# A two-layer decoder trunk on one core: another weight tile on the second queue, constants loaded later, early inputs stored without gaps, and a new hand-laid order

## The chip, the core and the metric

The kernel runs on one core of a Trainium2 chip. Its engines work side by side, each through its own instruction queue: PE (TensorE, matmuls; the profile shows its weight loads apart, as PEld), DVE (VectorE), ACT (ScalarE), POOL (GpSimd) and SP (SyncE), which issues nearly all transfers; ACT issues three. The metric is the device time of one execution in microseconds (us). Before the change the median of three runs is 358.94 us (358.47 to 359.08).

## What is computed

One sequence of 256 tokens of width 1,024 goes through two layers in float32. Layer 0 is block-sparse attention (with 256 tokens there is one block, so it is causal attention over 16 heads of 64), layer 1 is attention with a compressed, a selected and a window branch. Each layer has one input projection that also gives a SiLU gate, an output projection, and a gated per-layer embedding:

```
for i in range(DEPTH):                       # DEPTH = 2
    h = rms_norm(x, norm_gain[i])
    x = x + (moba_layer if i == 0 else nsa_layer)(h, ...)
    gate = sigmoid(rms_norm(x, ple_gate_gain[i]) @ ple_w_gate[i])
    x = x + gate * (p[i] @ ple_w_proj[i])

def moba_layer(h, w_in, q_gain, k_gain, w_out, pos):
    q, k, v, z = split(h @ w_in, 4)          # 1024 columns each
    q, k = rope(rms_norm(q, q_gain), pos), rope(rms_norm(k, k_gain), pos)
    return (attention(q, k, v) * silu(z)) @ w_out
```

## The kernel before

**Split matmuls.** The product of a float32 weight tile and the activations is made of three matmuls of type float32r. ACT (or DVE) copies a raw weight tile to `hi`, rounded; DVE subtracts, `lo = raw - hi`. The activation tile is split likewise, into the two halves of a tile `a`. Then PE adds hi x hi, hi x lo and lo x hi up in PSUM (`mul`, line 544). So a weight tile must be loaded, copied by ACT and subtracted by DVE before PE can use it whole; the matmuls with `hi` can run while `lo` is made.

**The start of the program.** The first unit of work is the queries of heads 0 to 7, `c0` to `c7`: one tile of 128 x 512 weights for each of the eight k-tiles of x (128 features each). Beside them run the first four k-tiles of the keys of the same heads, `d0` to `d3`, from the same activations. Each tile is two token halves of three matmuls of 512 columns, six in all; `c0` is loaded in two halves of 256 columns and takes twelve of half the width. `x0` to `x7` are the steps that load a k-tile of x (line 892) and split it, scaled by the gain; `w:c0` and so on load and split weights (lines 898 and 949); `c0`, `d0` and so on are the matmuls (lines 918 and 954). Steps `a.1` to `a.7` square the x tiles for the norm (ACT) and add the squares (DVE); `consts` loads the first constants and the gains of the heads, from which `tq` and `tk` make tables on DVE. Twenty matmuls on a constant (line 870) run first, while nothing has landed.

SP issues most transfers. ACT issues three before its first computation: the gains `gain_in`, the second half of c0's weights, and a third one, kept in the variable `second` (lines 883 and 884), which is `c1`.

**What sets the order.** The kernel is written as named steps. `PROGRAM` (line 25) is a list of step names, an order found by a search outside the kernel; it tells the order in which the steps are recorded and in which buffers are handed out. `Plan.schedule` (line 272) then deals the recorded operations to the engines: of those that are ready, each engine takes the one that can start first by a table of costs, and on equal times the one recorded first; a plain copy may go to ACT or DVE. For transfers this table holds an issue time, a lag and a rate by time of landing (`ISSUE, LAG, RATE`, line 242), and at most eight may be open (line 244). `hold` (line 262) keeps an operation until another one has been dealt; `BEHIND` (line 54) names the weight steps behind which the first constants and the rest of them are held. The instructions of each engine then run strictly in that order on the chip, each waiting on semaphores. All of them are issued from line 408, so every row of the profile carries that line, and tiles are told apart by name.

Raw tiles of the early steps lie in the five buffers `tmp` (shared with the squares of the norm and other short-lived values) or, from the fifth k-tile on, in pairs in the seven buffers `raw`; `hi` and `lo` have five buffers each, and `mm` is the PSUM of the projections.

Of the kernel before, what the change touches and what calls it, by code (L numbers as in the profile page):

```python
# [13 lines left out]
P = 128  # L14
T = 256
D = 1024
KT = 8
# [7 lines left out]
PROGRAM = ("x0 w:c0 x1 w:c1 w:d0 c0 x3 d0 x5 w:d1 c1 x2 consts w:c2 x4 w:d2 a.1 w:c3 c2 c3 x6 x7 w:c5 a.3 w:c4 c4 w:d3 a.5  "  # L25
# [28 lines left out]
BEHIND = "d0 k.2"  # L54
# [56 lines left out]
class Plan:  # L111
# [130 lines left out]
    ISSUE, LAG, RATE = 450.0, 2250.0, ((5000.0, 255.0), (9000.0, 340.0), (1e9, 400.0))  # L242
# [187 lines left out]
def trunk(ctx: ExitStack, tc: tile.TileContext, a, out):  # L430
# [28 lines left out]
    def load_consts(lo, hi):  # L459
        nc.sync.dma_start(cst[:, lo:hi], a["cst"][:, lo:hi])  # L460
# [258 lines left out]
    def tail(i, oT, pvs, zin, xz, norm):  # L719
# [21 lines left out]
        def load_p():  # L741
            pT = tmp("p").rearrange("p (k t) -> p k t", k=2)
            nc.sync.dma_start(pT, a["p"][:, i])
            for k in range(2):
                px[k] = split_act(pT[:, k])
# [130 lines left out]
    uq0 = Unit(a["moba_in"][0], False, x0)  # L876
    uq0.ps = [bank("mm", 4) for _ in range(2)]

    nc.sync.dma_start(xT[:, 0], a["x"][:, 0])
    halves = [load(a["moba_in"][0, 0, :, 0:256], 256, True)]  # L880
    since = len(nc.ops)
    nc.scalar.dma_start(gain_in, a["gain_in"])
    halves.append(load(a["moba_in"][0, 0, :, 256:512], 256, True, nc.scalar))
    second = load(a["moba_in"][0, 0, :, 512:1024], 512, True, nc.scalar)
# [7 lines left out]
    def first_x(k):  # L892
        if k:
            nc.sync.dma_start(xT[:, k], a["x"][:, k])
        x0[k] = split_act(xT[:, k], ng[:, 0, k:k + 1], k == 0)
        lows[k] = len(nc.ops) - 1

    def first_w(k):
# [4 lines left out]
        c0, raw = 512 * (k % 2), second if k == 1 else None  # L903
        if k >= 4:
# [4 lines left out]
            nc.sync.dma_start(raw, a["moba_in"][0, k // 2, :, c0:c0 + 512])  # L909
        since = len(nc.ops)  # L910
        uq0.w[k] = split(a["moba_in"][0, k // 2, :, c0:c0 + 512], (1, 512), small=k < 4, raw=raw)
# [525 lines left out]
def _arrays(i):  # L1437
    import numpy as np

    def c(v):  # L1440
        return np.ascontiguousarray(v)

    def feat(v):
        return c(v.reshape(KT, P, T).transpose(1, 0, 2))
# [92 lines left out]
```

## Time and profile before

| what | value |
|---|---|
| median of three runs | 358.94 us |
| profiled execution | 358.19 us |
| its span, first to last instruction | 356.4 us |
| PE busy | 349.5 us, 98% |
| weight loads busy | 305.6 us, 86% |
| DVE busy | 323.6 us, 91% |
| ACT busy | 276.8 us, 78% |
| granted TensorE clock | 1.000 |
| read from memory | 57.46 MB, 164 GB/s over the span |

A row of the timeline reads: start in us, length in us, engine, line, operation, the tiles written and read, shapes, how many are merged in the row, and in brackets the idle time before it and what ended it. A row of the groups has busy time and mean length after the bar. A row of the transfers gives size and the us from issue to landing. The profiled execution is 0.75 us shorter than the median of the runs. The end of a matmul is modelled, and the next one starts before it.

### The profile page before, as it was taken

Reading aid. Unit: us, or ns where it says so; the run is one execution under the profiler, and the core shown is the slowest. Engines: PE = TensorE matmul, PEld = TensorE weight load, DVE = VectorE, ACT = ScalarE, POOL = GpSimd, SP = SyncE. Lnnn points to the kernel's source line nnn. Section 1 sums busy time; section 2 is a strip of 40 time slices with the busy share of each in tenths; the row PEclk is TensorE's granted clock in tenths of the full one; section 3 lists DMA queues with packets and bytes.
Section 4 is the critical chain, followed back from the end, with each engine's and each line's share of the span. In section 5 each row is a group of like instructions: output and inputs, shape, how many; then the busy total and the mean of one; then the engine's idle time right before and its main releaser. Section 6 shows DMA issues by size and latency. Waiting matters only on the chain.

```text
span 356.4 us, 6657 instructions
## 1 busy us (share of the span) xinstructions
PE 349.5 (98%) x2315; PEld 305.6 (86%) x2315; DVE 323.6 (91%) x789; ACT 276.8 (78%) x613; POOL 28.0 (8%) x22
## 2 busy tenths in 40 slices
PE   7999999999999999999999999999999999999995
PEld 5788788989999888999889999877998888888884
DVE  3999899999999989889999999999999999979715
ACT  4875599999999986556854789979989999926721
POOL 1013403005000000000003300012000000000000
PEclk9999999999999999999999999999999999999999
DMA  7999376554534315653554865347653211352003
GB/s 219 318 410 387 124 255 231 176 179 166 160 109 145 123 59 164 203 171 114 166 183 142 269 237 179 124 161 259 232 157 102 95 59 62 91 183 81 0 2 118
DMA packets 20769, 58.94 MB, mean 165 GB/s; under 512 B 2560, under 2 KB 5632, under 8 KB 20736
## 3 DMA queue, kind: packets, MB, share of 16 engines
q1 hardware_dynamic: 20160, 58.04, 48.3%
q10 hardware_dynamic: 576, 0.48, 0.4%
q8 instruction: 18, 0.29, 0.3%
q14 instruction: 15, 0.12, 0.1%
HBM read 57.46 MB, written 1.05 MB: 164 GB/s over the span
## 4 chain that ended last, share of the span: by engine, by line
PE 93%; DVE 2%; ACT 2%; DMA 2%; issue 0%; DVEq 0%; ACTq 0%
PE mm L408 68%; PE tr L408 14%; PE s L408 10%; DMA xT<-in_x 1%; DMA gain_in<-in_gain_in 1%; DVE lo L408 1%; ACT hi L408 0%; DVE hl L408 0%; DVE pc L408 0%; DVE big L408 0%; ACT hl L408 0%; ACT sm L408 0%; ACT pt L408 0%; ACT vcB L408 0%; ACT tmp L408 0%; DVE tmp L408 0%
## 5 line engine op out<-in xcount | busy, mean ns | idle before, releaser
L408 PE MATMUL mm<-hi,a 128*128 128x512 f32 (+2 forms) x448 | 128.2, 375 | 1.9 <-ACT sqacc L408 1.2
L408 ACT ACTIVATE hi<-raw 128x1024 fp32r<-128x1024 f32 (+2 forms) x98 | 97.5, 1006 | 32.8 <-PE mm L408 21.6
L408 DVE TENSOR_TENSOR lo<-raw,hi 128x1024 fp32r<-128x1024 f32 (+2 forms) x98 | 112.4, 1160 | 6.9 <-ACT hi L408 6.6
L408 PE MATMUL mm<-a,hi 128*128 128x256 f32 (+1 forms) x512 | 107.8, 300 | 0.0
L408 PEld LDWEIGHTS mm<-hi,a 128*128 128x128 f32 x448 | 79.3, 189 | 15.7 <-ACT a L408 1.6
L408 PEld LDWEIGHTS mm<-a,hi 128*128 128x128 f32 x512 | 81.8, 190 | 2.5 <-ACT big L408 0.2
L408 PE MATMUL mm<-a,lo 128*128 128x256 f32 x288 | 80.5, 287 | 0.0
L408 PE MATMUL mm<-lo,a 128*128 128x512 f32 (+2 forms) x224 | 80.1, 370 | 0.0
L408 PEld LDWEIGHTS mm<-a,lo 128*128 128x128 f32 x288 | 54.4, 190 | 1.9 <-issue 0.3
L408 PEld LDWEIGHTS mm<-lo,a 128*128 128x128 f32 x224 | 41.9, 188 | 7.1 <-DVE lo L408 0.2
L408 ACT ACTIVATE sm<-sm,nb 128x128 f32<-128x128 f32 (+1 forms) x96 | 42.6, 448 | 2.2 <-DVE nb L408 1.6
L408 DVE CUSTOM_DVE_ANT_0 sm<-s,cst,nr_q 128x128 f32<-128x128 f32 (+1 forms) x80 | 32.0, 422 | 0.5 <-PE tr L408 0.2
L408 PE MATMUL tr<-cst,sm 128*128 128x128 f32 x144 | 23.3, 274 | 0.1
L408 ACT ACTIVATE pt<-tr 128x384 f32<-128x384 f32 x48 | 21.8, 483 | 1.0 <-PE tr L408 0.7
L408 POOL TENSOR_TENSOR r_q<-r,neg_half 128x16 f32<-128x16 f32 x5 | 16.1, 3216 | 70.9 <-DVE r L408 70.9
L408 ACT ACTIVATE a<-xT,gain_in 128x256 fp32r<-128x256 f32 x31 | 14.6, 497 | 8.5 <-DVE xT L408 5.2
L408 PEld LDWEIGHTS tr<-cst,sm 128*128 128x128 f32 x144 | 17.1, 140 | 2.4 <-ACT pt L408 0.4
L408 ACT ACTIVATE sm<-sm,l 128x128 f32<-128x128 f32 (+1 forms) x44 | 17.3, 442 | 1.5 <-DVE l L408 1.3
L408 ACT ACTIVATION_READ_ACCUMULATOR sm<-sm,nb 128x1 f32 x96 | 18.3, 191 | 0.0
L408 POOL TENSOR_TENSOR rstd<-ms,neg_half 128x2 f32<-128x2 f32 x4 | 3.2, 791 | 191.9 <-DVE ms L408 191.9
L408 PE MATMUL s<-a,hi 128*128 128x512 f32 (+1 forms) x64 | 18.0, 342 | 0.0
L408 DVE TENSOR_TENSOR hl<-tr,hl 64x512 fp32r<-64x512 f32 x24 | 16.5, 689 | 0.7
(188 smaller groups left out, 509.1 us busy)
## 6 DMA issues: line engine op xcount, KB each, us to landing
raw<-in_moba_in SPq DMA_DIRECT2D x26, 512.0 KB, 5.1
raw<-in_nsa_in SPq DMA_DIRECT2D x24, 512.0 KB, 4.3
raw<-in_w_out SPq DMA_DIRECT2D x16, 512.0 KB, 3.6
raw<-in_ple_gate SPq DMA_DIRECT2D x16, 512.0 KB, 3.5
raw<-in_w SPq DMA_DIRECT2D x8, 512.0 KB, 3.6
raw<-in_ple_proj SPq DMA_DIRECT2D x4, 512.0 KB, 3.9
tmp<-in_moba_in SPq DMA_DIRECT2D x6, 256.0 KB, 4.5
raw<-in_nsa_vs SPq DMA_DIRECT2D x4, 304.0 KB, 3.2
```

Of the source, the lines that this page charges most:

```text
L408: getattr(getattr(self.nc, o.engine), o.method)(*[real(x) for x in o.args], **{k: real(x) for k, x in o.kwargs.items()})
```

## The change

There are four edits.

1. The third transfer on ACT's queue, `second`, is now tile `d0` (keys, used with x0) and no longer `c1` (queries, used with x1). `c1` is loaded by SP like the other tiles.
2. The first constants are held behind the loading of `c2` (`BEHIND`) and no longer behind that of `d0`.
3. The host stores the early inputs piece by piece: each k-tile of x, each early weight tile of 128 x 512, the halves of `c0`, the two parts of the constants and the embeddings' tiles each lie in one run of memory. Before, a row of a piece was followed by a gap (1 KB rows every 8 KB for x, 2 KB rows every 4 KB for the tiles). What lands in the core is the same.
4. The rates in the cost table are lower early (230 bytes per ns up to 7 us where there were 255 up to 5 us), and `PROGRAM` is another order throughout.

```diff
-PROGRAM = ("x0 w:c0 x1 w:c1 w:d0 c0 x3 d0 x5 w:d1 c1 x2 consts w:c2 x4 w:d2 a.1 w:c3 c2 c3 x6 x7 w:c5 a.3 w:c4 c4 w:d3 a.5  "
+PROGRAM = ("x0 w:c0 w:d0 x1 w:d1 x3 c0 d0 x2 w:c1 w:c2 consts x4 w:c3 c1 tq w:d2 a.1 x5 d1 w:c4 a.3 w:d3 x7 c2 w:c5 x6 c3  "
...
-BEHIND = "d0 k.2"
+BEHIND = "c2 k.2"
...
-    ISSUE, LAG, RATE = 450.0, 2250.0, ((5000.0, 255.0), (9000.0, 340.0), (1e9, 400.0))
+    ISSUE, LAG, RATE = 450.0, 2250.0, ((7000.0, 230.0), (9000.0, 330.0), (1e9, 390.0))
...
-        nc.sync.dma_start(cst[:, lo:hi], a["cst"][:, lo:hi])
+        nc.sync.dma_start(cst[:, lo:hi], a["cst1" if lo else "cst0"])
...
-    second = load(a["moba_in"][0, 0, :, 512:1024], 512, True, nc.scalar)
+    second = load(a["tiles"][8], 512, True, nc.scalar)
...
-            nc.sync.dma_start(xT[:, k], a["x"][:, k])
+            nc.sync.dma_start(xT[:, k], a["x"][k])
...
-        c0, raw = 512 * (k % 2), second if k == 1 else None
-        if k >= 4:
+        c0 = 512 * (k % 2)
+        if k < 4:
+            raw = load(a["tiles"][k], 512, True)
+        else:
...
-            u.w[f"d{k}"] = split(a["moba_in"][2, k // 2, :, 512 * (k % 2):512 * (k % 2) + 512], (1, 512), small=True)
+            u.w[f"d{k}"] = split(a["tiles"][8 + k], (1, 512), small=True,
+                                 raw=None if k else second)
...
-    r["x"] = feat(i["x"][0].T)
+    r["x"] = c(i["x"][0].T.reshape(KT, P, T))
...
+    w = i["moba_w_in"][0]
+    r["first"] = np.stack([w[:P, 256 * h:256 * h + 256] for h in range(2)])
+    r["tiles"] = np.concatenate([w[:, 0:512].reshape(KT, P, 512), w[:4 * P, 1024:1536].reshape(4, P, 512)])
```

What this does to the instructions is shown at three places, all in the first 13 us. In the rows, `tmp_0` and `tmp_1` hold the halves of c0 at first and `tmp_2` the third transfer on ACT's queue; `hi_2` and `lo_2` are made of it; `a2_0` is x0 and `a2_1` is x1; `mm_0` and `mm_1` are the sums of the queries, `mm_2` and `mm_3` those of the keys.

First SP's transfers, behind x0 and the first half of c0. Before:

```order
L408 DMA xT_0_63<-in_x 128x256
L408 DMA tmp_3_78<-in_moba_in 128x512
L408 DMA xT_0_63<-in_x 128x256 x2
L408 DMA tmp_4_79<-in_moba_in 128x512
L408 DMA xT_0_63<-in_x 128x256
L408 DMA cst_0_65<-in_cst 128x384
L408 DMA gains_0_66<-in_head_gain 128x256
L408 DMA tmp_0_75<-in_moba_in 128x512
L408 DMA xT_0_63<-in_x 128x256
L408 DMA tmp_1_76<-in_moba_in 128x512
```

Now:

```order
L408 DMA xT_0_63<-in_x 128x256
L408 DMA tmp_3_78<-in_tiles 128x512
L408 DMA xT_0_63<-in_x 128x256 x2
L408 DMA tmp_4_79<-in_tiles 128x512
L408 DMA xT_0_63<-in_x 128x256 x2
L408 DMA tmp_0_75<-in_tiles 128x512
L408 DMA cst_0_65<-in_cst0 128x384
L408 DMA gains_0_66<-in_head_gain 128x256
L408 DMA tmp_1_76<-in_tiles 128x512
```

The sizes are the same up to the fifth k-tile of x; a sixth k-tile stands where the constants were, and the constants and the gains go behind the next weight tile (`tmp_0`, which is c2 now). `tmp_3` was d0 and is d1; `tmp_4` was d1 and is c1.

Then PE, from the last two matmuls of c0 on. Before:

```order
L408 MATMUL mm_0_71<-lo_1_117,a2_0_102 128x256
L408 MATMUL mm_1_72<-lo_1_117,a2_0_102 128x256
L408 MATMUL mm_0_71<-hi_2_113,a2_1_103 128x512
L408 MATMUL mm_1_72<-hi_2_113,a2_1_103 128x512
L408 MATMUL mm_0_71<-hi_2_113,a2_1_103 128x512
L408 MATMUL mm_1_72<-hi_2_113,a2_1_103 128x512
L408 MATMUL mm_2_73<-hi_3_114,a2_0_102 128x512 x2
L408 MATMUL mm_3_74<-hi_3_114,a2_0_102 128x512 x2
L408 MATMUL mm_2_73<-lo_3_119,a2_0_102 128x512
L408 MATMUL mm_3_74<-lo_3_119,a2_0_102 128x512
L408 MATMUL mm_0_71<-lo_2_118,a2_1_103 128x512
L408 MATMUL mm_1_72<-lo_2_118,a2_1_103 128x512
```

Now:

```order
L408 MATMUL mm_0_71<-lo_1_117,a2_0_102 128x256
L408 MATMUL mm_1_72<-lo_1_117,a2_0_102 128x256
L408 MATMUL mm_2_73<-hi_2_113,a2_0_102 128x512 x2
L408 MATMUL mm_3_74<-hi_2_113,a2_0_102 128x512 x2
L408 MATMUL mm_2_73<-lo_2_118,a2_0_102 128x512
L408 MATMUL mm_3_74<-lo_2_118,a2_0_102 128x512
L408 MATMUL mm_2_73<-hi_3_114,a2_1_103 128x512 x2
L408 MATMUL mm_3_74<-hi_3_114,a2_1_103 128x512 x2
L408 MATMUL mm_2_73<-lo_3_119,a2_1_103 128x512
L408 MATMUL mm_3_74<-lo_3_119,a2_1_103 128x512
L408 MATMUL mm_0_71<-hi_4_115,a2_1_103 128x512 x2
L408 MATMUL mm_1_72<-hi_4_115,a2_1_103 128x512 x2
```

PE went from c0 to c1 (x1), with d0 (x0) between c1's two parts; it now goes from c0 to d0, which needs x0 alone, then d1 and c1.

Last ACT and DVE, which feed these tiles. ACT before, from the copy of c0's second half on:

```order
L408 ACTIVATE hi_1_112<-tmp_1_76 128x256
L408 ACTIVATE a2_1_103<-xT_0_63,gain_in_0_64 128x256
L408 ACTIVATE sqacc_0_70<-xT_0_63 128x512
L408 ACTIVATE hi_3_114<-tmp_3_78 128x512
L408 ACTIVATE a2_2_104<-xT_0_63,gain_in_0_64 128x256
L408 ACTIVATE a2_3_105<-xT_0_63,gain_in_0_64 128x256
L408 ACTIVATE hi_4_115<-tmp_4_79 128x512
```

ACT now:

```order
L408 ACTIVATE hi_1_112<-tmp_1_76 128x256
L408 ACTIVATE a2_1_103<-xT_0_63,gain_in_0_64 128x256
L408 ACTIVATE sqacc_0_70<-xT_0_63 128x512
L408 ACTIVATE a2_2_104<-xT_0_63,gain_in_0_64 128x256
L408 ACTIVATE a2_3_105<-xT_0_63,gain_in_0_64 128x256
L408 ACTIVATE tmp_3_78<-xT_0_63 128x512
L408 ACTIVATE hi_4_115<-tmp_4_79 128x512
L408 ACTIVATE a2_4_106<-xT_0_63,gain_in_0_64 128x256
L408 ACTIVATE a2_5_107<-xT_0_63,gain_in_0_64 128x256
L408 ACTIVATE hi_0_111<-tmp_0_75 128x512
```

DVE now, over the same stretch:

```order
L408 CAST hi_2_113<-tmp_2_77 128x512
L408 TENSOR_TENSOR lo_2_118<-tmp_2_77,hi_2_113 128x512
L408 SCALAR_TENSOR_TENSOR a2_1_103<-xT_0_63,gain_in_0_64,a2_1_103 128x256
L408 CAST hi_3_114<-tmp_3_78 128x512
L408 TENSOR_TENSOR lo_3_119<-tmp_3_78,hi_3_114 128x512
L408 SCALAR_TENSOR_TENSOR a2_2_104<-xT_0_63,gain_in_0_64,a2_2_104 128x256
L408 SCALAR_TENSOR_TENSOR a2_3_105<-xT_0_63,gain_in_0_64,a2_3_105 128x256
L408 TENSOR_TENSOR sqacc_0_70<-sqacc_0_70,tmp_3_78 128x512
L408 TENSOR_TENSOR lo_4_120<-tmp_4_79,hi_4_115 128x512
```

The copy of `tmp_3` to `hi_3` went from ACT to DVE, and a square of the norm, which is written into `tmp_3` again, now stands on ACT ahead of the copy of `tmp_4`. The counts of operations on the engines stay nearly the same: DVE has one more copy of 512 columns and ACT one less, and three scalings of softmax rows and one copy out of PSUM change sides too.

More of the change, by code (lines that the diff above doesn't have):

```diff
@@ L742, in load_p @@
             pT = tmp("p").rearrange("p (k t) -> p k t", k=2)
-            nc.sync.dma_start(pT, a["p"][:, i])
+            nc.sync.dma_start(pT, a["p"][i])
             for k in range(2):
@@ L874, in trunk @@
     x0 = {}
-    uq0 = Unit(a["moba_in"][0], False, x0)
+    uq0 = Unit(None, False, x0)
     uq0.ps = [bank("mm", 4) for _ in range(2)]
-    nc.sync.dma_start(xT[:, 0], a["x"][:, 0])
-    halves = [load(a["moba_in"][0, 0, :, 0:256], 256, True)]
+    nc.sync.dma_start(xT[:, 0], a["x"][0])
+    halves = [load(a["first"][0], 256, True)]
     since = len(nc.ops)
     nc.scalar.dma_start(gain_in, a["gain_in"])
-    halves.append(load(a["moba_in"][0, 0, :, 256:512], 256, True, nc.scalar))
-    second = load(a["moba_in"][0, 0, :, 512:1024], 512, True, nc.scalar)
+    halves.append(load(a["first"][1], 256, True, nc.scalar))
+    second = load(a["tiles"][8], 512, True, nc.scalar)
     nc.scalar.activation(consts.tile([P, 16], F32, name="early"), neg_half, AF.Exp)
@@ L908, in first_w @@
             raw = pair[k // 2][:, c0:c0 + 512]
-            nc.sync.dma_start(raw, a["moba_in"][0, k // 2, :, c0:c0 + 512])
+            nc.sync.dma_start(raw, a["tiles"][k])
         since = len(nc.ops)
-        uq0.w[k] = split(a["moba_in"][0, k // 2, :, c0:c0 + 512], (1, 512), small=k < 4, raw=raw)
+        uq0.w[k] = split(None, (1, 512), small=k < 4, raw=raw)
         if k == 1:
@@ L934, in __init__ @@
             self.early, n = {}, "1" * h
-            self.u = {"k": Unit(a["moba_in"][2 + h], False, x0).steps(n + "k"),
-                      "v": Unit(a["moba_in"][4 + h], False, x0).steps(n + "v"),
-                      "q": Unit(a["moba_in"][1], False, x0).steps("1q") if h else uq0}
+            self.u = {"k": Unit(a["moba_in"][1 + h], False, x0).steps(n + "k"),
+                      "v": Unit(a["moba_in"][3 + h], False, x0).steps(n + "v"),
+                      "q": Unit(a["moba_in"][0], False, x0).steps("1q") if h else uq0}
             if not h:
@@ L1078, in trunk @@
         todo[f"next.{k}"] = lambda k=k: next_x(k)
-    tail(0, oT, pvs, [a["moba_in"][6 + h] for h in range(2)], x0, n0)
+    tail(0, oT, pvs, [a["moba_in"][5 + h] for h in range(2)], x0, n0)
     pe = consts.tile([P, 2, 16], F32, name="pe")
@@ L1441, in c @@
         return np.ascontiguousarray(v)
-    def feat(v):
-        return c(v.reshape(KT, P, T).transpose(1, 0, 2))
     def units(w, cols):
@@ L1458, in _arrays @@
     r = {}
-    r["x"] = feat(i["x"][0].T)
-    r["p"] = c(i["p"][:, 0].transpose(0, 2, 1).reshape(2, 2, P, T).transpose(2, 0, 1, 3))
+    r["x"] = c(i["x"][0].T.reshape(KT, P, T))
+    r["p"] = c(i["p"][:, 0].transpose(0, 2, 1).reshape(2, 2, P, T).transpose(0, 2, 1, 3))
     r["gain_in"] = c(np.concatenate([gains(i["norm_gain"]), gains(i["ple_gate_gain"])], 1))
-    r["moba_in"] = units(i["moba_w_in"][0], [s(512 * u) for u in range(8)])
+    w = i["moba_w_in"][0]
+    r["first"] = np.stack([w[:P, 256 * h:256 * h + 256] for h in range(2)])
+    r["tiles"] = np.concatenate([w[:, 0:512].reshape(KT, P, 512), w[:4 * P, 1024:1536].reshape(4, P, 512)])
+    r["moba_in"] = units(w, [s(512 * u) for u in range(1, 8)])
     w = i["nsa_w_in"][0]
@@ L1474, in _arrays @@
     r["w2"] = c(i["nsa_cmp_w2"][0].reshape(2, 2, P, HD).transpose(2, 1, 0, 3))
-    r["cst"] = _constants()
+    r["cst0"], r["cst1"] = (c(v) for v in np.split(_constants(), [384], 1))
     return r
```

42 rows, old and new, of the table PROGRAM are left out of this document.

## The prediction

> **What bounds the kernel now.** I read the page first, then a table of windows over the whole span, then the timeline of the first 16 us engine by engine, then the transfers. The page names the bound:
>
> ```profile
> span 356.4 us, 6657 instructions
> PE 349.5 (98%) x2315; PEld 305.6 (86%) x2315; DVE 323.6 (91%) x789; ACT 276.8 (78%) x613; POOL 28.0 (8%) x22
> PE 93%; DVE 2%; ACT 2%; DMA 2%; issue 0%; DVEq 0%; ACTq 0%
> ```
>
> PE (TensorE) is busy 98% of the span, and 93% of the chain that ended last is PE's own work. The change alters no count of matmuls, so it can only take PE's idle time away or add to it. The windows say where that idle time is (columns: window, its length, then busy us of PE, PEld, DVE, ACT, POOL, the clock, DMA share, GB/s):
>
> ```profile
> 0.00:4.85 4.85, 4.08 (x20) 2.85 (x21) 1.38 (x5) 2.22 (x4) 1.01 (x7) 1.00 0.53 143
> 4.85:7.90 3.05, 1.84 (x14) 1.65 (x13) 0.85 (x3) 1.01 (x2) 0.00 (x0) 1.00 1.03 361
> 7.90:12.70 4.80, 4.34 (x18) 3.29 (x18) 4.29 (x10) 3.54 (x9) 0.00 (x0) 1.00 0.81 244
> 14.30:60.00 45.70, 45.70 (x214) 37.15 (x214) 44.10 (x85) 35.42 (x60) 8.46 (x6) 1.00 0.80 298
> 60.00:100.00 40.00, 40.00 (x274) 36.94 (x273) 39.35 (x89) 38.74 (x86) 6.94 (x2) 1.00 0.48 160
> 100.00:140.00 40.00, 39.84 (x304) 35.29 (x303) 37.89 (x105) 35.44 (x86) 0.00 (x0) 1.00 0.37 119
> 266.00:280.00 14.00, 13.77 (x116) 11.57 (x116) 13.57 (x45) 12.49 (x33) 0.00 (x0) 1.00 0.45 149
> 330.00:356.40 26.40, 22.41 (x124) 19.28 (x122) 13.53 (x26) 10.52 (x23) 0.70 (x1) 1.00 0.13 40
> ```
>
> From 14.3 us on PE is never idle for more than an instant: only the stretches 100:140 and 266:280 lose 0.16 and 0.23 us, and the 4 us at the very end are the last gate, its store and nothing that the change touches. So there are two stops to win, both before 13 us (start, length, engine):
>
> ```profile
> 0.77 4.42 PE L408 MATMUL tr<-const-bfloat16-1.0 128*128 128x256 bf16 x20 [0.77 <-PEq L1526]
> 4.85 0.88 PE L408 MATMUL mm<-hi,a 128*128 128x256 f32 x4
> 6.29 0.40 PE L408 MATMUL mm<-lo,a 128*128 128x256 f32 x2
> 7.92 2.08 PE L408 MATMUL mm<-hi,a 128*128 128x512 f32 x8 [1.23 <-ACT sqacc L408]
> 11.88 0.39 PE L408 MATMUL mm<-lo,a 128*128 128x512 f32 x1
> 12.74 1.21 PE L408 MATMUL mm<-hi,a 128*128 128x512 f32 x4 [0.48 <-ACT hi L408]
> 13.79 0.63 PE L408 MATMUL mm<-lo,a 128*128 128x512 f32 x2
> 14.25 1.13 PE L408 MATMUL mm<-hi,a 128*128 128x512 f32 x4
> 14.18 0.53 PEld L408 LDWEIGHTS mm<-hi,a 128*128 128x128 f32 x3 [0.20 <-ACT hi L408]
> ```
>
> The twenty warm-up matmuls end as tile c0's begin at 4.85, so c0 itself cannot come sooner. After it PE stops 1.23 us before c1, and 0.48 us before the fourth tile; 0.2 us more is lost at 14.2. (A 512-wide matmul starts 0.23 us after the one before: two of them lie between 13.79 and 14.25. The shown gaps are therefore a little short, since an end is modelled.) A tile of six such matmuls is 1.38 us. That 1.9 us, plus 0.4 in the two later windows, is all that can be won: some 2.3 us.
>
> **What the first stop waits for.**
>
> ```profile
> 7.34 0.43 DVE L408 CAST hi<-tmp 128x512 fp32r<-128x512 f32 x1 [2.20 <-DMA tmp<-in_moba_in]
> 7.69 0.48 DVE L408 SCALAR_TENSOR_TENSOR a<-xT,gain_in,a 128x256 fp32r<-128x256 f32 x1
> 8.08 1.31 DVE L408 TENSOR_TENSOR lo<-tmp,hi 128x512 fp32r<-128x512 f32 x2
> 6.89 0.51 ACT L408 ACTIVATE a<-xT,gain_in 128x256 fp32r<-128x256 f32 x1 [2.23 <-DMA xT<-in_x]
> 12.06 0.63 ACT L408 ACTIVATE hi<-tmp 128x512 fp32r<-128x512 f32 x1 [1.15 <-PE mm L408]
> tmp<-in_moba_in ACTq DMA_DIRECT2D x1, 256.0 KB, 5.7
> tmp<-in_moba_in SPq DMA_DIRECT2D x1, 256.0 KB, 4.2
> ```
>
> The wait is labelled with ACT's square, but the square has nothing to do with c1: c1's raw weights, ACT queue's third transfer, issued at 1.65, land 5.7 us later, at 7.3; DVE casts them 7.34 to 7.77 and PE starts 0.12 us behind. x1 was there first (ACT took it at 6.89). So the later of the two was the weights. The second stop is likewise a landing, not PE, as ACT's row at 12.06 has it: the fourth tile's weights were issued at 7.78 and land 4.2 us later, at 12.0.
>
> **The change, part by part.** *Third transfer.* It now carries d0 (key weights for x0) in the place of c1. Same queue, same size, the same three transfers ahead of it: by this row it lands at 7.3 again, and PE starts at 7.9 again. The edit frees the start from x1, which was not the last to come. Worth here: 0.
>
> *What follows on PE, walked with the durations above.* The order is now d0, d1, c1. DVE: cast of d0 7.34 to 7.77, its lo 7.8 to 8.5 (0.69 for one: the pair took 1.31), low part of x1 to 8.9, cast of d1 to 9.25, its lo to 9.95. PE: d0 7.9 to 9.28, d1 from 9.37 (cast plus 0.12) to 10.75. Then c1's copy to hi, on ACT: it now stands behind a square that writes the buffer of d1's raw weights, so it waits until DVE's lo of d1 is read out at 9.95.
>
> ```profile
> 12.99 0.61 ACT L408 ACTIVATE tmp<-xT 128x512 f32<-128x512 f32 x1
> 13.52 0.61 ACT L408 ACTIVATE hi<-tmp 128x512 fp32r<-128x512 f32 x1
> 10.10 0.69 DVE L408 TENSOR_TENSOR lo<-tmp,hi 128x512 fp32r<-128x512 f32 x1
> ```
>
> By these rows square and copy are 0.53 apart and 0.61 long: square 10.05, copy 10.58 to 11.2, c1 on PE 11.27 to 12.65. So half a microsecond of the stop comes back here, as a wait for ACT. Before, the same tiles with the second stop behind them took until 12.74. Gain 0.1, and up to 0.3 if the 0.2 at 14.2 goes too: I take **0.2 us**.
>
> *Constants behind the third tile.* SP stops issuing at 4.71 and goes on at 7.34, when ACT's third transfer has landed (the longest of its waits for a landing, 2.2 us, last number of its row):
>
> ```profile
> SPq L408 <- DMA tmp<-in_moba_in: 3.2, 5, 2.2
> 4.71 0.43 SPq L408 DMA_DIRECT2D cst<-in_cst  x1
> 7.34 0.33 SPq L408 DMA_DIRECT2D gains<-in_head_gain  x1
> gains<-in_head_gain SPq DMA_DIRECT2D x1, 128.0 KB, 4.0
> ```
>
> Now c2 is the one issued at 7.34, without 128 KB of gains ahead of it, so it is there by 11.5 at the latest (4.2 us after issue, as when the gains were ahead); ACT comes to it at 11.9, behind c1's copy and two of x, and has it done at 12.55, 0.1 before PE wants it. This removes the landing as the cause of the second stop; what is late instead is ACT, which the walk counts already. If the cover goes, PE waits as long as c2 lands behind 11.9. The 192 KB of constants and 128 KB of gains now go ahead of c3's 256 KB: 576 KB, which at the 350 GB/s of the rates below take 1.6 us, from c2's landing near 11.4 to 13.0. With the copy's 0.61 c3 is ready at 13.6, and PE wants it at 14.0. (If the gains move at the 140 GB/s of 8 to 10.5 us, that is 0.5 more and a stop of 0.1.) I take none. The tables that use the constants stand on DVE, behind the lo of c2 (13.3), a microsecond after the gains; nothing on PE waits for them in the first 20 us.
>
> *Pieces without gaps.* The packets keep their size, since a row of a partition is still 1 or 2 KB. The rate in half-microseconds from 0 to 20 us says what the gaps cost:
>
> ```profile
> GB/s 0 0 0 29 193 314 305 238 176 227 322 354 377 401 390 317 163 125 102 180 135 320 346 381 383 387 352 371 361 324 340 377 377 385 315 315 410 438 418 418
> raw<-in_moba_in SPq DMA_DIRECT2D x1, 512.0 KB, 3.2
> ```
>
> With gaps the rate reaches 401 at 6.5 us and 387 at 12.5; without (from 18 us) about 418. So gaps cost some 4 to 8% of the 2.6 us that 1.04 MB need at 400: 0.1 to 0.2 us. From 3.5 to 5.0 it is only 238, 176 and 227; if gaps caused that, 380 there would bring (380 - 214) x 1.5 = 250 KB more, or 0.65 us at 380. Bounds 0 and 0.65. Against the upper end speaks the gap-free load alone at 60.9 us: its 512 KB take 3.2 us, hardly the pace of a stream. I take **0.2 us** for d0 and all behind it; the chain DVE, ACT, PE above moves along with it.
>
> [...]
>
> *The new order behind 20 us.* All steps are dealt anew, with equal matmuls, and DVE and ACT get almost equal work. With PE already without gaps it can give at most the 0.4 us named above; it can lose more. I take 0.
>
> Sum: 0.2 + 0.2 = **0.4 us** less. The profiled execution took 358.19 us, 1.79 of it outside the span, so it would be 357.8; it lies 0.75 under the median of the runs, 358.94. Against that median the forecast is **358.5 us**.
>
> **Rivals.**
>
> *B: the early transfers come at full rate.* If the slow 3.5 to 5.0 us were the gaps, d0 lands at 6.65, casts, and PE starts at 7.25; d1, c1 and SP's next issues come 0.65 sooner too. With the 0.2 of the walk and the 0.4 of the later windows: 1.25 less, 357.7. For it: PE starts 0.6 us behind that landing and waits for nothing else then. Against: strided pieces at 401 two microseconds later.
>
> *C: DVE becomes the bound where it is full.* In 60:100 DVE is busy 39.35 of 40.00 us, so there is 0.65 us of room. A new order that puts tiles on PE sooner than their lo, or lets other DVE work in ahead of them, decides against the kernel once more than that is pushed ahead of a tile. One such lo costs, by the mean in
>
> ```profile
> L408 DVE TENSOR_TENSOR lo<-raw,hi 128x1024 fp32r<-128x1024 f32 (+2 forms) x98 | 112.4, 1160 | 6.9 <-ACT hi L408 6.6
> ```
>
> 1.16 us. One out of place is 1.16, less the 0.65 of room and the 0.4 won at the start: no change. From the second on the kernel is slower, and two are 2.32 - 0.65 - 0.4 = 1.3 more, 360.2. For it: PE's work after 14 us has no gaps to give, so another order has almost only losses open to it. Against: the order before keeps PE fed at this DVE load over 250 us, and the work on DVE is nearly the same.
>
> *D: the first edit only trades waits.* If d1, which SP issues right behind x1, lands 0.5 later than the transfer in its place does now, the chain of cast, lo, square and copy passes it on whole: 0.5 - 0.4, about 359.0, no change.
>
> **How the numbers follow.** My forecast with its own range 358.1 to 358.9: 0.43. B 0.31, C 0.18, D 0.08. A measurement of this kernel tells 0.2% (0.72 us) from no change. Faster by more than that: B, and 0.08 of the forecast's faster edge, 0.39. Slower: C and a little of D, 0.22. Within: 0.39. The range reaches below B's 357.7 by half a microsecond for a gain of both, and to C: 357.2 to 360.2; it leaves out about 2 in 10.
>
> **What would show it.** The cast of d0 on DVE at 7.3 and PE's second block at 7.9 say that the third transfer comes as before; a start near 7.2 says B. A wait of PE of about 0.5 us near 10.8, released by ACT's copy of c1, shows the walk right; no such wait shows it wrong. Landing of c2 before 11.9 shows the constants' step right; a stop at 14.0 shows c3 late. PE idle in 60:100 or 200:266, where it now has none, is C. The prediction is wrong if the time leaves its range, or if PE's gaps before 15 us change by more than 1 us in either direction.

## The result and the profile after

| kernel, chip | median us | range of the runs | ratio to before, 95% interval |
|---|---|---|---|
| before, first chip | 359.0 | 358.47 to 360.0 (6 runs) | |
| changed, first chip | 356.91 | 356.72 to 357.88 (6 runs) | 0.9943 (0.9926 to 0.9960) |
| before, another chip | 359.46 | 358.24 to 360.63 (11 runs) | |
| changed, that chip | 357.1 | 356.66 to 357.98 (6 runs) | 0.9938 (0.9916 to 0.9960) |

The kernel became 2.1 us faster on the first chip and 2.4 on the other, where 0.4 was forecast; 356.91 lies 0.3 under the predicted range. On the four chips of the experiments below, 17 of the 56 runs of the kernel before show a granted clock of 0.995 and take 359.9 to 360.7 us, which no run of another kernel does (why is open, since none of them was profiled); without them its medians are 358.8 to 359.0, and the gain on the other chip is 1.8 us. The profiled execution after the change took 356.72 us. Its page:

```profile
span 354.9 us, 6666 instructions
PE 348.7 (98%) x2315; PEld 305.2 (86%) x2315; DVE 323.8 (91%) x788; ACT 277.0 (78%) x614; POOL 28.0 (8%) x22
PE 90%; ACT 4%; DMA 3%; DVE 2%; issue 0%; ACTq 0%; DVEq 0%
```

PE's work is the same; its share of the chain fell from 93 to 90%, and transfers have 3%. Up to 13.42 us the chain now holds no matmul: it goes through the landing of d0, then through a weight tile that SP issued at 7.04 (start, length):

```profile
7.04 5.62 DMA tmp<-in_tiles
13.42 2.79 PE mm L408 x11
```

Before, the chain had PE's work in it from 7.93 us on. PE's timeline there (start, length, and in brackets the idle time ahead and what ended it):

```profile
0.77 3.79 PE L408 MATMUL tr<-const-bfloat16-1.0 128*128 128x256 bf16 x20 [0.77 <-PEq L1529]
6.09 1.19 PE L408 MATMUL mm<-hi,a 128*128 128x512 f32 x4
7.64 1.16 PE L408 MATMUL mm<-hi,a 128*128 128x512 f32 x4
9.46 1.19 PE L408 MATMUL mm<-hi,a 128*128 128x512 f32 x4 [0.19 <-ACT hi L408]
10.95 1.08 PE L408 MATMUL mm<-hi,a 128*128 128x512 f32 x4
13.42 1.65 PE L408 MATMUL mm<-hi,a 128*128 128x512 f32 x6 [0.93 <-ACT hi L408]
```

The tiles are d0, d1, c1, c2, and from 13.42 c3 with d2. d0 starts at 6.09; before, the second block came at 7.92. c1 waits a little for ACT's copy, as the walk had it. The first constants no longer stand ahead of c2, which follows without a stop. But 0.93 us are lost ahead of c3. What it waits for (ACT, DVE and SP rows of the timeline, then rows of the transfers: size, us from issue to landing):

```profile
12.74 1.28 ACT L408 ACTIVATE hi<-tmp 128x512 fp32r<-128x512 f32 x2 [1.47 <-DMA tmp<-in_tiles]
11.88 0.49 DVE L408 TENSOR_TENSOR tq<-cst,gains 128x128 f32<-128x128 f32 x2 [0.26 <-DMA gains<-in_head_gain]
6.04 0.43 SPq L408 DMA_DIRECT2D cst<-in_cst  x1
6.51 0.43 SPq L408 DMA_DIRECT2D gains<-in_head_gain  x1
tmp<-in_tiles ACTq DMA_DIRECT2D x1, 256.0 KB, 3.9
cst<-in_cst SPq DMA_DIRECT2D x1, 192.0 KB, 4.4
gains<-in_head_gain SPq DMA_DIRECT2D x1, 128.0 KB, 5.3
GB/s 0 0 0 111 219 219 287 307 391 391 336 391 406 318 236 331 341 235 177 143 131 195 326 369 385 397 389 408 389 389 379 389 385 397 389 438 410 418 410 410
```

ACT queue's third transfer, issued at 1.65, takes 3.9 us and not 5.7. The constants land at 10.4, the 128 KB of gains at 11.8, and c3 behind them at 12.66. From 8.5 to 11 us only 131 to 235 GB/s arrive (the last row has one number for each half microsecond).

Matmul by matmul (each one's start against the durations of all that PE did ahead of it) the two profiles compare as in the first row of this table, in us; a minus is a lead over the first profile of the kernel before. The columns count PE's work and not time: 14 us of work are done some 16 us after the start. The other rows are runs told below, each one profile.

```
PE's work done, us          14      30     100     120    end
changed                  -0.80   -0.83   -0.76   -1.39  -1.38
changed, once more       +0.49   +0.46   +0.54   -0.10  -0.11
changed, with gaps       -0.95   -1.02   -0.93   -1.58  -1.60
changed, equal rows      -1.22   -1.27   -1.19   -1.82  -1.80
changed, no early stops  -2.18   -2.24   -2.15   -2.79  -2.82
before, second profile   +0.58   +1.21   +1.07   +1.07  +1.08
before, third profile    +0.60   +0.72   +0.57   +0.60  +0.59
before, no gaps          -0.30   -0.30   -0.44   -0.45  -0.48
old order, repaired      -1.71   -1.72   -1.84   -1.86  -1.80
the same, once more      -1.27   -1.27   -1.39   -1.39  -1.38
```

Two things can be read off it: the leads at 14 us of work differ by 2.8 us, and from 30 us on each order adds its own constant, -0.5 to -0.6 in the new, -0.1 to -0.2 in the old.

### The profile page after: what moved, and what is told of

The parts are those of the page before. It is cut to its first block, busy times and chain, and to the rows that moved or that the text cites. A ratio compares the mean times of both kernels' runs of the same rounds, so it can differ in the third digit from the quotient of the medians.

```text
span 354.9 us, 6666 instructions
## 1 busy us (share of the span) xinstructions
PE 348.7 (98%) x2315; PEld 305.2 (86%) x2315; DVE 323.8 (91%) x788; ACT 277.0 (78%) x614; POOL 28.0 (8%) x22
## 4 chain that ended last, share of the span: by engine, by line
PE 90%; ACT 4%; DMA 3%; DVE 2%; issue 0%; ACTq 0%; DVEq 0%
PE mm L408 66%; PE tr L408 14%; PE s L408 10%; DMA tmp<-in_tiles 3%; ACT hl L408 1%; ACT hi L408 1%; DVE lo L408 1%; ACT tmp L408 1%; ACT pt L408 1%; ACT sm L408 0%; DVE pc L408 0%; ACTq L408 0%; DVE big L408 0%; ACT vcB L408 0%; DVE tmp L408 0%
## 5 line engine op out<-in xcount | busy, mean ns | idle before, releaser
L408 PE MATMUL mm<-a,lo 128*128 128x256 f32 x288 | 79.6, 285 | 0.0
L408 ACT ACTIVATE a<-xT,gain_in 128x256 fp32r<-128x256 f32 x31 | 14.5, 501 | 6.8 <-DVE xT L408 5.5
L408 POOL TENSOR_TENSOR r_q<-r,neg_half 128x16 f32<-128x16 f32 x5 | 14.6, 2922 | 63.9 <-DVE r L408 63.9
L408 DVE TENSOR_TENSOR hl<-tr,hl 64x512 fp32r<-64x512 f32 x24 | 16.5, 689 | 0.9 <-ACT hl L408 0.3
```

The costliest lines, as they stand in the source:

```text
L408: getattr(getattr(self.nc, o.engine), o.method)(*[real(x) for x in o.args], **{k: real(x) for k, x in o.kwargs.items()})
```

## Experiments

In some of the edits operations are taken out of the dealt order and put behind another one; `move(what, behind)` stands for that, and everything else keeps its place. Differences are against the median of the kernel before on the same chip.

**Is the kernel before as its first profile shows it?** It was profiled twice more, unchanged.

> The kernel before, unchanged, profiled once more: its first profiled execution (358.19 us) was the shortest of all its timed ones (median 359.1). If the landings differ from one execution to another (theory O): x1 and ACT queue's third transfer land at times that differ from 6.8 and 7.3 us by 0.5 us or more, and the time follows them. If the layout with gaps fixes them (theory P): they land within 0.3 us of 6.8 and 7.3 again, and what makes this execution longer lies elsewhere, as another idle time of PE.

> As the look before it: a third profiled execution of the kernel before. Theory O: landings of x1 and of the third transfer spread over 0.5 us or more in the three. Theory P: within 0.3 us of 6.8 and 7.3 in all three.

359.28 and 358.77 us. PE's timeline in the second profile, with the late landing behind it, and last the same stop in the third:

```profile
7.24 2.10 PE L408 MATMUL mm<-hi,a 128*128 128x512 f32 x8 [0.54 <-DVE hi L408]
13.33 1.20 PE L408 MATMUL mm<-hi,a 128*128 128x512 f32 x4 [1.73 <-ACT hi L408]
21.14 0.51 PE L408 MATMUL mm<-hi,a 128*128 128x512 f32 x1 [0.38 <-ACT hi L408]
11.96 0.49 DVE L408 TENSOR_TENSOR tk<-cst,gains 128x128 f32<-128x128 f32 x2 [0.76 <-DMA gains<-in_head_gain]
gains<-in_head_gain SPq DMA_DIRECT2D x1, 128.0 KB, 5.2
13.37 1.21 PE L408 MATMUL mm<-hi,a 128*128 128x512 f32 x4 [1.58 <-ACT hi L408]
```

The third transfer lands at 6.64 and 6.83 us (7.32 in the first profile), and the stop ahead of the fourth tile, 0.48 us there, is 1.73 and 1.58 here: the gains come 2.4 us behind the constants (1.2 there), and c2 at 12.6 behind them. In the second profile PE stops once more at 20.8, for a weight tile. So both theories got a part: the landing of the third transfer does vary, but it came earlier here and the time was longer, so the time does not follow it; the excess over the first profile lies mostly at the gains. The first profile, from which the forecast was made, was a lucky one in just the stop that the second edit removes.

**Gaps back in the changed kernel, and gaps in the weights alone.**

```diff
-            nc.sync.dma_start(xT[:, k], a["x"][k])
+            nc.sync.dma_start(xT[:, k], a["x"][:, k])
...
-            raw = load(a["tiles"][k], 512, True)
+            raw = load(a["tiles"][k // 2, :, c0:c0 + 512], 512, True)
```

(and so for the other early pieces; the second kernel has only the lines of the weights)

> The changed kernel with one part undone: the early inputs (x, the early weight tiles, the constants, the embeddings' tiles) are stored with gaps again, as before the change. The order of the instructions on every engine is that of the changed kernel. Theory P (the gaps are what made the early transfers slow): ACT queue's third transfer lands near 7.3 us again, as before the change, and not at 5.6; PE's second block starts near 7.9 and not at 6.1; the time is 1.0 to 1.8 us above the changed kernel's, about 358.0 to 358.7. Theory O (the landings differ from one execution to another whatever the layout, and the gain is that of the new order): the third transfer lands within 0.4 us of 5.6, and the time is within 0.4 us of the changed kernel's 356.9.

> The changed kernel with gaps in the early weight tiles alone (rows of 1 or 2 KB every 4 KB); x (1 KB rows that lay 8 KB apart before) and the constants stay without gaps, and the order is that of the changed kernel. If the rows of the weights are what the memory is slow at: third transfer near 7.3 us, time as with all gaps (358.0 to 358.7 under theory P). If the rows of x are: third transfer near 5.6 us, time within 0.3 us of 356.9. If both share it: in between. Theory O: near 5.6 and 356.9.

With all gaps 356.9 us, 2.25 under before: ratio 0.9933 (0.9920 to 0.9947), the changed kernel's. With the weights' gaps 357.17: 0.9938 (0.9923 to 0.9953). In the new order the layout shows no worth in the total (the intervals are some 0.5 us to each side); theory O stands there. PE with all gaps:

```profile
6.15 1.20 PE L408 MATMUL mm<-hi,a 128*128 128x512 f32 x4
13.23 1.67 PE L408 MATMUL mm<-hi,a 128*128 128x512 f32 x6 [0.66 <-ACT hi L408]
```

c3 is again what PE waits for, at 13.23. In the other kernel the third transfer came late, at 6.99, d0 stopped PE 0.98 us (start at 7.49), and c3 began at 13.75 with no stop at all ahead of it: the first stop took the place of the second.

**The old order without gaps.** The kernel before with the third edit alone.

> The kernel before with one part of the change alone: the early inputs are stored without gaps; the order of the instructions on every engine, with c1 as ACT queue's third transfer and the constants where they were, is that of the kernel before. Theory P: c1 lands near 5.6 us and not at 7.3, PE's second block starts near 6.2, and the time falls by 1.0 to 1.8 us, to about 357.2 to 358.0; if it falls as far as 357.0 the new order is worth nothing. Theory O: the third transfer lands where it did, and the time is within 0.4 us of 359.0.

357.6 us, 1.55 under before: 0.9955 (0.9941 to 0.9970). Theory P, here. The third transfer lands at 6.04 and PE goes on at 6.64. SP resumes its issues, which wait for that landing, at 6.06 (7.34, 6.66 and 6.85 in the profiles of before), so the gains land at 11.0 and c2 at 11.7:

```profile
6.64 2.26 PE L408 MATMUL mm<-hi,a 128*128 128x512 f32 x8 [0.30 <-DVE hi L408]
12.46 1.21 PE L408 MATMUL mm<-hi,a 128*128 128x512 f32 x4 [1.30 <-ACT hi L408]
```

So one edit gains 1.5 us in one order and nothing that shows in the other. Over all runs the third transfer landed at 5.6 to 7.3 us with gaps in the weights (7 profiles, mean 6.6) and at 5.2 to 6.6 without (10 profiles, mean 5.8). In the old order alone the two do not overlap: 6.4 to 7.3 with gaps (5 profiles), 5.5 to 6.0 without (3). One landing shows the layout every time: x0, the first transfer of all, issued at 0.74, landed at 3.2 to 3.4 us in the six profiles with gaps in x, and at 2.8 to 3.0 in the eleven without.

**The second edit alone, in the old order.**

```diff
+    move([cst, gains], load of c2)
+    move(the two tk, lo of d2)
```

> The kernel before with the second edit alone: the first constants and the gains are issued behind c2's weights and not ahead of them, and the two small table operations that read them stand 3 operations later on DVE; nothing else is moved, and the inputs keep their gaps. If c2 behind the gains is what made the second stop: c2 lands by 11.3 us and not at 11.97, the stop of 0.5 us ahead of the fourth tile is gone or under 0.2, and the time is 0.3 to 0.6 us under 359.1. Rival: ACT's copy stays late for another cause, or a later tile waits as long; the stop moves and the time stays within 0.3 us of 359.1.

357.8 us, 1.14 under before: 0.9963 (0.9951 to 0.9975). c2 lands at 9.45 and runs without a stop; the stop is now ahead of the tile behind the gains:

```profile
11.19 1.07 PE L408 MATMUL mm<-hi,a 128*128 128x512 f32 x4
13.59 2.03 PE L408 MATMUL mm<-hi,a 128*128 128x512 f32 x7 [0.88 <-ACT hi L408]
```

The stop moved one tile on and shrank; the rival's half of it is true as well.

**Are the gains slow because one row is read 128 times?**

```diff
-load_consts(0, 384), load_gains(gmoba, 0, 2)
+load_consts(0, 384), nc.sync.dma_start(gmoba, a["gains0"])
...
+    r["gains0"] = c(np.broadcast_to(r["head_gain"].reshape(-1)[:4 * HD], (P, 4 * HD)).reshape(P, 2, 2, HD))
```

> The changed kernel with one transfer read from another layout: the gains of the heads, 1 KB that were read 128 times over (once for each partition), lie in memory as 128 equal rows of 1 KB. Same 128 KB, same order of all instructions. If the repeated reading of one row is what makes this transfer slow (it landed 1.35 us behind the constants ahead of it, 97 GB/s): it lands 0.4 to 0.6 us behind them, c3 lands near 11.8 us and not at 12.66, PE's stop ahead of c3 shrinks from 0.9 to 0.2 us or less, and the time is 0.3 to 0.8 us under the changed kernel's, 356.1 to 356.6; nothing if, as when the constants were moved, a later wait takes the gain. Rival (128 packets of 1 KB take that long whatever they read, or the queue is short of issued transfers there): lands 1.2 us or more behind, stop and time as in the changed kernel, 356.9.

> The kernel before with one transfer read from another layout: the gains of the heads as 128 equal rows of 1 KB in memory, where one row was read 128 times; the same order, and the gaps of all other inputs stay. In its two later profiled executions the gains landed 2.4 us behind the constants ahead of them, c2 at 12.6, and PE stopped 1.6 to 1.7 us ahead of the fourth tile. Theory T (the first 20 us are set by the stream of transfers, and the slow gains stand in it ahead of c2): gains 0.4 to 0.8 us behind the constants, c2 at 11.0 to 11.6, that stop 0.5 to 0.9, and the time 0.8 to 1.5 us under 359.0. Rival (the slow place is the halt of SP's issues behind the late third transfer, not the gains): gains fast, but c2 no earlier than 12.2, the time within 0.4 us of 359.0.

In the changed kernel 356.55 us: 0.9930 (0.9908 to 0.9952); in the kernel before 358.32: 0.9971 (0.9957 to 0.9986), 0.75 less. The gains now land 0.47 and 0.34 us behind the constants. Changed kernel with equal rows:

```profile
gains<-in_gains SPq DMA_DIRECT2D x1, 128.0 KB, 3.4
13.00 1.66 PE L408 MATMUL mm<-hi,a 128*128 128x512 f32 x6
GB/s 0 0 0 59 251 307 246 219 287 313 379 383 399 387 344 275 348 353 284 279 250 246 270 309 320 332 393 369 402 402 395 426 406 381 434 418 410 401 401 418
```

Eleven profiles with the one row show 1.0 to 2.7 us between the two landings, six with equal rows 0.34 to 0.47. That is shown, and from 8.5 to 11 us 246 to 353 GB/s arrive here, where the changed kernel had 131 to 235. In the total of the old order it brings a little less than was expected: c2 came at 11.0 and its stop shrank to 0.4, but two stops of 0.3 and 0.6 opened at 14 and 16.5, on the tiles behind. In the new order c3 landed at 12.23 and not at 11.8, with 0.2 us left of the stop ahead of it. That is 1.8 us behind the gains and 2.3 behind the constants, no less than in the changed kernel's first profile (2.2; 3.4 in its second): part of the delay went over to c3, while the constants themselves came 0.5 us earlier (9.94). The gain of 0.36 is smaller than the spread of either kernel's runs.

**Constants and gains much later.** Behind c6, eleven transfers on; then the same with equal rows.

```diff
+    move([cst, gains], load of c6)
+    move(tq and tk, lo of c6)
```

> The changed kernel with 192 KB of first constants and 128 KB of gains issued eleven transfers later, behind the weights of c6, and the four small table operations that read them 5 to 8 us later on DVE; nothing else is moved. Theory S (the stop of PE near 12.5 us is the fourth query tile landing late behind those 320 KB): c3 lands at 11.0 to 11.3 us and not at 12.66, PE's stop ahead of it (1.0 us) is gone or under 0.2, and the time is 0.7 to 1.0 us under the changed kernel's, about 356.0. Rival: PE catches up on a later wait in any case (the trace shows it nearly without idle time from 14 us on only because it is late); then the stop goes, another of the same length opens before 30 us (a landing or DVE), and the time is within 0.3 us of 356.9.

> The changed kernel with both: constants and gains issued behind c6, their tables 5 to 8 us later on DVE, and the gains as 128 equal rows. Theory T: with the constants late alone the stop moved to 28 us, where PE waited 1.0 us behind a weight tile that landed 2.5 us behind the one ahead of it; the gains' second and more of slow reading no longer lies in the stream, so that stop is under 0.4 us, and the time is 356.0 to 356.4, under both the changed kernel (356.9) and the one with equal rows alone (356.55). Rival: the stop at 28 us is the order of DVE and ACT behind the moved tables, not a landing; it stays near 1 us, and the time is 356.8 to 357.4.

357.27 us (0.9943; 0.9925 to 0.9962) and 357.04 (0.9937; 0.9917 to 0.9956): no gain over the changed kernel in either. c3 lands at 10.25 and 10.48, the stop ahead of it is gone, and PE stops later:

```profile
29.46 0.70 PE L408 MATMUL mm<-hi,a 128*128 128x512 f32 x2 [1.02 <-DVE tmp L408]
```

with one row, and with equal rows

```profile
25.63 0.43 PE L408 MATMUL tr<-cst,rstd 128*128 128x128 f32 x2 [0.33 <-POOL rstd L408]
```

In the first row PE waits for DVE's `tmp`, and DVE works without a break from 25 us to there; so its late work behind the moved tables, which the rival named, has a part in that stop. With equal rows the stop at 28 us went, as theory T had it, but the norm's `rstd`, whose sums stand on DVE behind the moved tables, held PE at 25 us (0.5 us by the starts of the matmuls); of a lead of 1.00 us at 14 us of work 0.25 is left at 30. The total is the rival's.

**Does c1's wait for ACT cost what it shows?**

```diff
+    move([square a.3], copy of c1)
+    move([its add], lo of c1)
```

> The changed kernel with ACT's copy of c1 ahead of the square that waits for DVE's lo of d1, and DVE's lo of c1 ahead of the add that reads that square; nothing else moved. By the prediction's walk PE's wait for c1 near 9.4 us (0.36 us of idle time) is then gone. Theory T (the stream of transfers sets the start): the wait goes, the stop ahead of c3 grows by as much, and the time is within 0.2 us of 356.9. Rival W (each stop of PE at the start is paid in full): 0.3 to 0.4 us less, 356.5 to 356.6.

357.17 us: 0.9938 (0.9916 to 0.9959). The wait is gone, and the stop ahead of c3 is longer:

```profile
9.60 1.09 PE L408 MATMUL mm<-hi,a 128*128 128x512 f32 x4
14.05 1.66 PE L408 MATMUL mm<-hi,a 128*128 128x512 f32 x6 [1.16 <-ACT hi L408]
```

Part of that is this execution's own late gains (2.6 us behind the constants). Nothing was won, as T expects (its band ended at 357.1); 0.36 less (W) would be 356.55, inside the spread of the runs, 356.48 to 357.77, so the time alone does not decide.

**The old order with all repairs, the new order with all repairs.** The old one without gaps, with constants and gains behind c2 and equal rows; c1 is still ACT queue's third transfer. The new one with equal rows, constants and gains behind d2 (tq behind the lo of c4), and c1's copy ahead of the square.

> The kernel before, in its own order, with the early inputs without gaps, the constants and gains behind c2, and the gains as 128 equal rows: everything that was seen to speed the transfers of the first 20 us, and c1 still as ACT queue's third transfer. Theory T: the new order gives only what the traces show behind 20 us (0.55 us: 0.3 between 30 and 40 us, 0.6 between 100 and 120, less 0.35 between 40 and 100), so this one is 0.5 to 0.7 us above the changed kernel with equal rows: 357.0 to 357.3. Rival (the new order of the first 14 us, d0 as third transfer among it, is worth as much again): 357.6 or more. Rival (the gain behind 20 us is not the order's): 356.6 or less.

> The changed kernel, in its new order, with the stops of its start taken out: the gains as 128 equal rows, constants and gains behind d2 (two tiles later), their first two table operations behind the lo of c4, and ACT's copy of c1 ahead of the square. Theory M (the total is the start of c3 plus a rest that the order alone sets, and the new order's rest is 0.55 us shorter): PE begins c3 at 12.3 to 12.6 us, the rest from there is 341.3 to 341.7 us as in the profiles of the changed kernel, and the time is 355.6 to 356.1, under the old order with the same repairs by 0.3 to 0.7. Rival N (behind 20 us PE runs into the same later limits, whatever it wins ahead of them): the rest grows by what the start won, a new stop of 0.4 us or more opens before 30 us, and the time is 356.4 to 356.9.

> The old order with the inputs without gaps, the constants and gains behind c2 and the gains as equal rows, beside the changed kernel on the same chip. Theory M: 356.2 to 356.6. Its first profile had no stop of PE behind 6.5 us. Rival N makes no other forecast here; if it is within 0.2 us of the changed kernel with its stops taken out, the new order's work behind 20 us is not worth its 0.55 us in the total.

> The changed kernel, unchanged, for a comparison on one chip. 356.7 to 357.1; PE's stop ahead of c3 0.7 to 1.3 us, c3 at 12.3 to 13.3 us behind the gains, and from PE's start of c3 to the end of the span 341.3 to 341.7 us.

The old order: 356.35 us (0.9922; 0.9897 to 0.9948), and 356.69 (0.9924; 0.9901 to 0.9947) on the chip of the other two. There the new order with its stops taken out came to **355.83 us**, 0.9903 (0.9881 to 0.9925), under both kernels of this study, and the changed kernel to 357.1. It is 0.86 under the old order, where 0.3 to 0.7 was expected, but these two intervals overlap. The windows of the new order with repairs (length, then busy us of PE and PEld):

```profile
4.85:14.30 9.45, 9.45 (x48) 8.14 (x47) 9.07 (x20) 7.30 (x15) 0.00 (x0) 1.00 1.04 369
```

PE is busy for all of 4.85 to 14.3. The same window of the kernel before, in its second profile:

```profile
4.85:14.30 9.45, 7.18 (x36) 5.68 (x35) 6.33 (x14) 5.45 (x12) 0.00 (x0) 1.00 0.96 315
```

where 2.27 us are idle. The changed kernel's other execution shows how far the gains can go the other way, 2.7 us behind the constants:

```profile
13.32 0.49 DVE L408 TENSOR_TENSOR tq<-cst,gains 128x128 f32<-128x128 f32 x2 [1.25 <-DMA gains<-in_head_gain]
14.71 1.66 PE L408 MATMUL mm<-hi,a 128*128 128x512 f32 x6 [1.74 <-ACT hi L408]
GB/s 0 0 0 66 259 319 219 252 262 305 385 352 389 391 363 307 364 288 158 77 110 162 252 277 311 387 399 397 385 375 348 266 326 348 299 291 311 352 397 295
```

From PE's start of c3 to the end of the span the new order needs 341.5 (the changed kernel, 354.9 - 13.42), 341.5 (once more, 356.2 - 14.71), 341.6 with gaps, 341.5 with equal rows, 341.6 with the copy moved, and 341.3 with all repairs (353.5 - 12.18): wherever c3 starts, the rest is the same. Three kernels have more: the one with gaps in the weights, 342.05, which stops again at 14.5, and the two with the constants behind c6, 342.9 and 342.2, whose later stops are told above. So theory M holds for the repaired kernel, and N does not: nothing behind 20 us took its lead back. A lead at the start can still be lost at a later stop, as the constants behind c6 show. The expectation for the old order failed in its size: 356.35 where 357.0 to 357.3 was expected, since its start was no worse than the changed kernel's with equal rows (-1.71 and -1.27 in its two profiles against -1.22 at 14 us of work). So the new order of the first 14 us shows no gain of its own. The second of these profiles has a stop that the first had not, ahead of a weight tile that landed at 12.87, when between 10.81 and 12.10 only 128 KB of x had landed; so the gains, which came 0.34 us behind the constants here, are not the only late landing:

```profile
13.63 1.19 PE L408 MATMUL mm<-hi,a 128*128 128x512 f32 x4 [0.73 <-ACT hi L408]
```

## Why the prediction was wrong

The forecast was 358.5 us and 356.91 was measured, 1.6 us less. Profile against profile 0.4 less was forecast and 1.47 was seen. Three steps failed. The start: a lead of 0.83 us at 30 us of PE's work, where 0.4 was forecast; d0 landed 1.74 us earlier, where 0.2 was taken, and a stop of 0.93 us ahead of c3, where none was taken, took part of it back. The new order behind it: 0.55 more, where nothing was (0.1 lies behind the last matmul). And the level: 0.75 us between the profiled execution and the median was added to the forecast, but the profile of the changed kernel lies 0.19 under its median, so 0.56 too much was added. The start's share hangs on the execution: in the other profile of the changed kernel it is 0.46 us behind and not 0.83 ahead, and the two later profiles of the kernel before are 0.72 and 1.21 behind.

**What bounds the kernel.** "So there are two stops to win, both before 13 us": the place was right, the size was not. The view was one execution; its own 0.75 us under the median was noted and then carried along as a constant offset. It was not one: the missing time lay mostly in the second stop, taken as 0.48 us and 1.58 and 1.73 in the later profiles, which the second edit acts on.

**Third transfer, worth 0.** Not contradicted. PE's second block starts 0.60 us behind that landing with c1 and 0.51 with d0, and the old order with c1 there, once repaired, starts no later than the changed kernel with equal rows. That the block starts at 6.09 and not at 7.9 comes from the landing.

**The walk over d0, d1, c1.** Its wait for ACT's copy behind the square came, 0.36 us where half a microsecond was said; with the wait taken out nothing was won, since PE then stopped longer ahead of c3. The 0.2 us that the walk was to gain are not seen.

**Constants behind c2.** That c2 would come in time was right (10.0). "c3 is ready at 13.6, and PE wants it at 14.0 ... I take none" failed, the other way: PE wanted c3 at 12.3, being earlier, and the 128 KB of gains moved at 50 to 100 GB/s (they landed 1.35 and 2.7 us behind the constants), under the 140 named there. The stop was 0.93 and 1.74 us. The gain of this edit was under-priced as well, since it was priced by the one short stop: alone, in the old order, it brings 1.14 us.

**Pieces without gaps, 0.2 us with bounds 0 and 0.65.** In the old order 1.55 us, in the new one 0: this edit has no price of its own. The third transfer came 0.8 us earlier on average (5.8 us against 6.6), above the upper bound of 0.65 that rival B took; the ranges of single executions overlap (5.2 to 6.6 and 5.6 to 7.3).

**The new order behind 20 us, 0 and at most 0.4.** It gives 0.4 to 0.45: from 30 us to the end five executions of the new order gain 0.53 to 0.58, five of the old lose none and gain 0.08 to 0.18. PE's busy time did not show it (19.84 us before and 19.91 now between 100 and 120 us), since the modelled ends (median length 0.28 us, where the starts lie 0.12 apart) fill short waits between matmuls; the starts do.

So of 2.1 us some 0.45 are the order's, and 1.65 are left for the start by subtraction. By edits, the second one alone in the old order (1.14) and the order behind 20 us make 1.6 of the 2.1; what the rest comes from stays open, and it is no more than the intervals allow. Rival B had the cause of its first part, early transfers, and even its 357.7 was not low enough. C did not happen: from 30 to 100 us of work the lead changes by 0.07. Nor did D: d1 landed 0.7 us behind d0, and the lead was kept.

## What to carry to other kernels

Take the profile of several executions before a start-up is priced: a stop that waits for a transfer can be 0.5 us in one and 1.7 in the next, and a single profile says which one it was only through its time against the median. Price such a start as one stream with one last landing: a stop removed ahead of it can come back there, as c1's did, and two edits that both shorten the stream need not add up (the layout brought 1.55 us in one order and nothing in the other). A row that all 128 partitions need landed 1.0 to 2.7 us behind the transfer ahead of it when it lay in memory once, and 0.34 to 0.47 when it lay there 128 times; in the total that brought 0.75 us in one order and no more than the spread of the runs in the other.

## What was not expected of the hardware

One row of 1 KB read 128 times landed 1.0 to 2.7 us behind the transfer ahead of it, 128 equal rows 0.34 to 0.47, and the whole stream fell meanwhile, to 77 GB/s in one half-microsecond of the changed kernel's second profile. Why the one row is slow, no run here shows.

The pace of PE at the start changes at another moment in each execution: its matmuls of 256 columns start 0.213 us apart at first and 0.11 to 0.12 later. By the starts of the matmuls it changes at some 3.65 us in the old order with the second edit alone, and at some 6.7 in the old order with repairs. The windows show a granted clock of 1.00 all the while, but the trace has no entry of the clock ahead of that moment: the first one, of 1.00, stands at 5.20 us in the first profile of before and at 3.74 in that of the change, in both between the last slow start and the first fast one. Twenty warm-up matmuls took 4.42 us in the first profile of before and 3.79 in that of the change, so c0, which the prediction held could not come sooner than 4.85, began at 4.36 there. With 4.42 the first matmuls of c0 can be slow too: in the old order with repairs

```profile
4.85 1.20 PE L408 MATMUL mm<-hi,a 128*128 128x256 f32 x4
6.28 0.82 PE L408 MATMUL mm<-hi,a 128*128 128x256 f32 x4
```

four of them take 1.20 us there, and took 0.74 after the change, where the pace had changed at 3.7 us:

```profile
4.36 0.74 PE L408 MATMUL mm<-hi,a 128*128 128x256 f32 x4
```

Once no landing stops PE any more, as in that run, this is what is left of the start: c1 began at 7.17 us, straight behind c0, where c0 was over by 6 us in the changed kernel. What sets the moment of the change was not tried; in these runs it came 2.9 to 5.9 us after PE's first matmul.
